# Bonus sums tied to steps of the block inverse's substitution, and a key layout in which one 128x128 transpose serves two heads

## The chip, the cores and the metric

The kernel runs on one core of a Trainium2 chip. The metric is the device time of one execution in microseconds; before the change three executions took 909.81, 911.17 and 912.35 us, median 911.17. A TensorE matmul engine (PE), VectorE (DVE), ScalarE (ACT), GpSimd (POOL) and SyncE (SP) each run a list of instructions in a fixed order and wait for each other through semaphores. ACT, POOL and SP also start DMA transfers from their lists.

## The reference

One block of a streaming encoder on 512 frames of 1024 channels, all in float32: an RWKV-7 branch and an RG-LRU branch from one input projection, merged by gates; then cross-attention into 256 memory frames; then a gated ConvFFN; RMSNorm in front of each and at the end. The change is in the RWKV-7 branch:

```python
def step(state, inp):
    r_t, w_t, k_t, v_t, a_t, b_t = inp
    sa = jnp.einsum('bhij,bhj->bhi', state, a_t)
    state = (state * w_t[:, :, None, :] + sa[..., None] * b_t[:, :, None, :]
             + v_t[..., None] * k_t[:, :, None, :])
    y_t = jnp.einsum('bhij,bhj->bhi', state, r_t)
...
y = ((y - mean) * lax.rsqrt(var + LNX_EPS)).reshape(bsz, s, A_WIDTH) * lnx_g + lnx_b
bonus = jnp.sum(r * k * r_k, axis=-1, keepdims=True) * v
return (y + bonus.reshape(bsz, s, A_WIDTH)) * g
```

There are 8 heads of 64 channels. `a_t` is minus the normalised key `kk`, and `b_t` is `kk * a`, where `a` is a sigmoid gate. The bonus of a head is a sum over its 64 channels of `r * k * r_k`, times `v`.

## The kernel before

**Precision.** A float32 weight is split into a high part (ACT copies it to a shorter format, L114) and a low part (DVE subtracts, L115), and each product is three matmuls (`mm3`, L160 to L162). `sum_exact` (L150 to L157) sums over the 64 channels of a head in the same way: ACT makes the high half, DVE the low half, and PE multiplies each by a matrix of blocks of ones into one PSUM bank.

**Staging.** Channels lie on the 128 partitions, frames along the free dimension. Two heads share a tile of 128 partitions: a pair; there are four pairs, each half of the partitions one head. The recurrence goes in 8 chunks of 64 frames.

1. The keys and values of the memory, and the norm of x, to about 57 us.
2. The input projection `in_proj` (`inproj`, L516): 38 blocks of 128 columns, 24 matmuls of 512 frames each. First the 14 blocks that RWKV-7 needs, then 24 others. From about 57 us PE takes these blocks, and what the other stages give it is put between them.
3. For each pair, between 100 and 195 us: `prep` and `prep2` make the decays, gates and normalised keys; the betas `kk*a` and the keys `k`, both divided by the running decay, are written into `KBt`; `scores` (L598) multiplies them by `AK` and masks the results into `BZ` and `AK`; the block of scores goes out to DRAM (`dM`). `bonus` (L585) forms `r*k*r_k`, sums it with `sum_exact`, multiplies by `vT`, adds the bias `lnx_b` and writes it out to DRAM (`dBo`), from where the group norm near the end of the branch reads it.
4. The inverse of a 32x32 triangular block for each head and chunk: `Nm` is loaded from `dM` on SP's queue (L654), and DVE substitutes in 31 steps (L656 to L661), each a product (L660, `zz`) and a reduction (L661, into `Zt`), from 212.45 to 253 us. The rest of the inverse follows with PE (`zh`, L687).
5. The loop over the chunks, from 285 to 343 us: `rows_kb` (L741) transposes the betas and keys of a chunk on PE, so that frames lie on the partitions, and ACT copies them out of PSUM; `chunk` (L753) uses them for the state's update.
6. Merge, cross-attention and FFN, to 900 us.

**Order.** A scheduler sets every engine's list when the kernel is built, by the priorities of the program. PE's matmuls of stage 4 and 5 are put between those of `in_proj`. A weight's raw data has four buffers, its high and low parts three each. SP's queue takes the loads of raw weights in turn, with the loads of stage 4 between them; a load waits until its buffer is free. GpSimd sums weights of the FFN in DRAM by DMA (`dS`), each of its transfers tied to a matmul of `in_proj`.

**Layout of KBt.** Each pair has 2·8 + 1 rows of 64 frames: row 1 + 2c holds the betas of chunk c for both heads, the rows after it the keys of the first head and the rows before it the keys of the second. So the 128 columns that belong together (`kb_cols`) begin at another row for each half of the partitions, and the two heads are transposed apart.

Of the kernel before, what the change touches and what calls it, by code (L numbers as in the profile page):

```python
# [53 lines left out]
def hybrid_block_kernel(ctx: ExitStack, tc: tile.TileContext, xT_d, mT_d, pv_d, cst_d, win_d, wk_d, wv_d,  # L54
# [423 lines left out]
    pa_ctx = ExitStack()  # L478
    pa = pa_ctx.enter_context(tc.tile_pool(name="pa", bufs=1, reuse_waits="tile"))
    BZ = pa.tile([P, NPAIR * NC, P], F32, tag="AR", name="BZ")  # L480
    KBt = big.tile([P, NPAIR, 2 * NC + 1, HD], F32, tag="x16", name="KBt")
    vT = pa.tile([P, NPAIR, T], F32, name="vT")
    AK = pa.tile([P, 2, NPAIR * NC, P], F32, tag="SC", name="AK")
    PC = pa.tile([P, NPAIR, NC], F32, name="PC")
# [76 lines left out]
    def prep2(j, pk, pr, at, Pi, Pp):  # L561
        c3 = lambda a: a.rearrange("p (c t) -> p c t", t=HD)
        kk = pp.tile([P, T], F32, tag="kk", name=f"kk{j}")
        S.activation(kk, pk, AF.Copy, scale=par("k_k", j))
        sq = pp.tile([P, T], F32, tag="q", name=f"sq{j}", bufs=2)
        S.activation(sq, kk, AF.Square)
        ps = rw_ps(f"ss{j}")
        sum_exact(ps, bonesr, sq, tp, "xb", f"ss{j}")
        tab.rsqrt(sq, ps, 1.0, eps[:, 2:3])
        V.scalar_tensor_tensor(kk, sq, 1e12, kk, ALU.min, ALU.mult)  # L570
        jc = slice(j * NC, (j + 1) * NC)
        for e in range(2):
            hs = half[e]
            V.scalar_tensor_tensor(AK[hs, e, jc, 0:HD], c3(kk)[hs], -1.0, Pp[hs, :, 0:HD], ALU.mult, ALU.mult)
        V.tensor_tensor(kk, kk, at, ALU.mult)
        V.tensor_tensor(KBt[:, j, 1::2, :], c3(kk), c3(Pi), ALU.mult)
        S.activation(at, at, AF.Identity, scale=par("k_a", j), bias=oka[:, j:j + 1])
        V.tensor_tensor(pk, pk, at, ALU.mult)
        V.tensor_tensor(KBt[0:HD, j, 2::2, :], c3(pk)[0:HD], c3(Pi)[0:HD], ALU.mult)
        V.tensor_tensor(KBt[HD:P, j, 0:2 * NC:2, :], c3(pk)[HD:P], c3(Pi)[HD:P], ALU.mult)  # L580
        for e in range(2):
            hs = half[e]
            V.tensor_tensor(AK[hs, e, jc, HD:P], c3(pr)[hs], Pp[hs, :, 1:], ALU.mult)

    def bonus(j, pk, pr):  # L585
        V.scalar_tensor_tensor(pr, pr, par("r_k", j), pk, ALU.mult, ALU.mult)
        ps = rw_ps(f"bo{j}")
        sum_exact(ps, bonesr, pr, tp, "xb", f"bo{j}")
        V.tensor_tensor(pr, ps, vT[:, j, :], ALU.mult)
        S.activation(pr, pr, AF.Identity, bias=par("lnx_b", j))  # L590
        nc.scalar.dma_start(dBo[j], pr)

    def kb_cols(j, e, c):
        return KBt[half[e], j, 2 * c + 1 - e:2 * c + 3 - e, :].rearrange("p a t -> p (a t)")

    def scores(j):  # L598
        for e in range(2):
            hs, oh = half[e], half[1 - e]  # L600
            for cg in range(2):
                ps = rw_ps(f"sc{j}_{e}_{cg}")
                i0 = j * NC + cg * 4
                for i in range(4):
                    PE.matmul(ps[:, i * P:(i + 1) * P], kb_cols(j, e, cg * 4 + i), AK[hs, e, i0 + i, :],
                              start=True, stop=True)
                p3 = ps.rearrange("p (c t) -> p c t", t=P)
                m3 = scmask.unsqueeze(1).to_broadcast([P, 4, P])
                V.tensor_tensor(BZ[hs, i0:i0 + 4, :], p3[hs], m3[hs], ALU.mult)
                V.tensor_tensor(AK[oh, e, i0:i0 + 4, :], p3[oh], m3[oh], ALU.mult)  # L610
            with tc.high_priority(offset=1000000):
                nc.sync.dma_start(dM[e * 32 + j * NC:e * 32 + (j + 1) * NC].rearrange("i s t -> s i t"),
                                  BZ[hs, j * NC:(j + 1) * NC, 0:HD])
# [7 lines left out]
    for jp in range(2):  # L621
        js = (2 * jp, 2 * jp + 1)
        pks, prs = {}, {}
        for j in js:
            pks[j] = pp.tile([P, T], F32, tag="pk", name=f"pk{j}", bufs=2)
            evac_shift(inproj(4 + j), 4 + j, pks[j])
        for j in js:
            prs[j] = pp.tile([P, T], F32, tag="pr", name=f"pr{j}", bufs=3)
            evac_shift(inproj(j), j, prs[j])
        for j in js:  # L630
            evac_shift(inproj(8 + j), 8 + j, vT[:, j, :])
        for j in js:
            if j == 3:
                for i in IN_REST[:NEARLY]:
                    gate_block(i - 22)
            at, L, Pp = prep(j)
            prep2(j, pks[j], prs[j], at, L, Pp)
            scores(j)
            bonus(j, pks[j], prs[j])

    pp_ctx.close()
    pq_ctx = ExitStack()
    pq = pq_ctx.enter_context(tc.tile_pool(name="pq", bufs=1, reuse_waits="tile"))
    YB = pq.tile([P, 4, T], F32, name="YB")


    with tc.tile_pool(name="pz", bufs=1, reuse_waits="tile") as pz:
        Nm = pz.tile([P, 32, 32], F32, name="Nm")
        Zt = pz.tile([P, 32, 32], F32, name="Zt")
        Zn = pz.tile([P, 32, 32], F32, name="Zn")  # L650
        zz = pz.tile([P, 31 * 31], F32, name="zz")
        with tc.high_priority(offset=1000000):
            for b in range(2):
                nc.sync.dma_start(Nm[b * HD:(b + 1) * HD], dM[:, b * 32:(b + 1) * 32, b * 32:(b + 1) * 32])  # L654
        V.memset(Zt, 0.0)
        V.memset(Zt.rearrange("p a b -> p (a b)")[:, 0:1024:33], 1.0)  # L656
        for s in range(30, -1, -1):
            n = 31 - s
            t3 = zz[:, 0:n * n].rearrange("p (a b) -> p a b", b=n)
            V.tensor_tensor(t3, Zt[:, s + 1:, s + 1:], Nm[:, s:s + 1, s + 1:].to_broadcast([P, n, n]), ALU.mult)  # L660
            V.tensor_reduce(Zt[:, s + 1:, s:s + 1], t3, AX.X, ALU.add)  # L661
        V.tensor_copy(Zn, Zt.rearrange("p a b -> p b a"))
        with tc.high_priority(offset=1000000):
            for b in range(2):
                nc.sync.dma_start(dZ[b], Zn[b * HD:(b + 1) * HD])
            nc.sync.dma_start(dZt, Zt[0:HD])
# [72 lines left out]
        return UV  # L739

    def rows_kb(c):  # L741
        KBr = ch.tile([P, 2, NPAIR, HD], F32, tag="KBr", name=f"KBr{c}", bufs=2)
        for e in range(2):
            ps = ch_ps(f"kbr{c}_{e}", ("kv", "s")[e])
            for j in range(NPAIR):
                PE.transpose(ps[:, j * HD:(j + 1) * HD], kb_cols(j, e, c), ident[half[e], half[e]])
            S.copy(KBr[:, e], j3(ps[:, 0:256]))
        return KBr

    def pc_b(c):  # L750
# [2 lines left out]
    def chunk(c, UV, KBr, SP):  # L753
# [22 lines left out]
        if not last:  # L776
            nUV = rows_v(c + 1)
            pss = ch_ps(f"s{c}", "s")
            for j in range(NPAIR):
                for e in range(2):  # L780
                    PE.matmul(pss[half[e], j * HD:(j + 1) * HD], KBr[:, e, j, :], UV[:, e, j, :],
                              start=True, stop=True)
        for j in range(NPAIR):
            for e in range(2):
# [633 lines left out]
```

## Time and profile before

| | us |
|---|---|
| median of three executions | 911.17 |
| the profiled execution | 909.73 |
| its span, from the first to the last instruction | 908.0 |
| PE busy | 890.5 (98%) |
| DVE busy | 687.4 (76%) |
| ACT busy | 510.4 (56%) |
| POOL busy | 129.3 (14%) |

The profile comes from one execution. "Busy" counts the time in which an engine runs at least one instruction; issuing a DMA does not count. In a timeline, "[0.35 <-DVE bo_l L155]" behind a row says that the engine was idle for 0.35 us before it, and that DVE's instruction of line 155 ended the wait. Matmuls overlap: the time between the starts of two in a row is less than the length of one. The granted clock of PE is 1.00 at 2.4 GHz and 0.50 at 1.2 GHz.

### The profile page before, as it was taken

To read this page: it belongs to the slowest core of one execution; us is meant where nothing else is said; L and a number is where in the kernel's file an instruction comes from. 1 tells how busy PE (TensorE), PEld (TensorE's weight loads), DVE (VectorE), ACT (ScalarE), POOL (GpSimd) and SP (SyncE) were. 2 spreads that over 40 slices of the span, in tenths; PEclk is the share of its full clock that TensorE was granted. 3 is DMA by queue.
4 is the path that set the end of the run, shared out by engine and by line. 5 is a ranking of instruction groups with operands and counts; after the bars stand their busy time and mean duration, and the time that the engine had idled before them with its cause. 6 is when DMAs were issued, how large, how long until landed. Compare 5 with 4: busy or idle time off the path is not lost. (4 is left out here: it accounts for less than half of the span.)

```text
span 908.0 us, 15914 instructions
## 1 busy us (share of the span) xinstructions
PE 890.5 (98%) x6218; PEld 776.1 (85%) x6218; DVE 687.4 (76%) x1096; ACT 510.4 (56%) x779; POOL 129.3 (14%) x159
## 2 busy tenths in 40 slices
PE   7999999999999999999999999999999999999996
PEld 6988877788877777887887778999999999999996
DVE  7884598776957585776565568788998888999674
ACT  6674675542236675234454446765665556767663
POOL 0102222010011212001112211111111111201100
PEclk9999999999999999999999999999999999999999
DMA  8878899667499749858788868898989998998963
GB/s 276 277 263 230 186 237 208 179 165 206 139 205 246 167 106 194 258 180 223 210 243 190 177 152 185 240 273 247 280 249 290 258 316 251 248 277 222 269 197 93
DMA packets 102411, 200.07 MB, mean 220 GB/s; under 512 B 25344, under 2 KB 36736, under 8 KB 102272
## 3 DMA queue, kind: packets, MB, share of 16 engines
q1 hardware_dynamic: 69504, 119.75, 41.0%
q0 software_dynamic: 25504, 67.38, 36.8%
q10 hardware_dynamic: 7328, 11.92, 3.9%
q8 instruction: 49, 0.80, 0.3%
q14 instruction: 26, 0.21, 0.1%
HBM read 187.75 MB, written 77.59 MB: 292 GB/s over the span
## 5 line engine op out<-in xcount | busy, mean ns | idle before, releaser
L126 ACT CAST wfi_h<-wfi_r 128x1024 fp32r<-128x1024 f32 x77 | 81.0, 1052 | 76.8 <-PE fx_ps L161 21.1
L160 PE MATMUL in_ps<-hT,win_h 128*128 128x512 f32 x304 | 121.9, 402 | 0.8 <-DVE pr L525 0.7
L162 PE MATMUL in_ps<-hT,win_l 128*128 128x512 f32 x304 | 120.8, 398 | 0.0
L161 PE MATMUL in_ps<-hT,win_h 128*128 128x512 f32 x304 | 120.6, 398 | 0.0
L127 DVE TENSOR_TENSOR wfi_l<-wfi_r,wfi_h 128x1024 fp32r<-128x1024 f32 x77 | 94.0, 1221 | 23.5 <-ACT wfi_h L126 23.3
L425 POOL DMA_DIRECT2D dS<-in_wfi x66 | 66.5, 1044 | 267.0 <-PE in_ps L160 132.4
L114 ACT CAST win_h<-win_r 128x1024 fp32r<-128x1024 f32 x38 | 39.8, 1048 | 71.9 <-PE in_ps L161 70.9
L115 DVE TENSOR_TENSOR win_l<-win_r,win_h 128x1024 fp32r<-128x1024 f32 x38 | 46.4, 1221 | 32.6 <-ACT win_h L114 32.5
L160 PEld LDWEIGHTS in_ps<-hT,win_h 128*128 128x128 f32 x304 | 57.0, 187 | 15.6 <-DVE pr L525 1.1
L161 PEld LDWEIGHTS in_ps<-hT,win_h 128*128 128x128 f32 x304 | 57.0, 188 | 14.0 <-issue 0.7
L162 PEld LDWEIGHTS in_ps<-hT,win_l 128*128 128x128 f32 x304 | 57.0, 187 | 13.9 <-issue 0.2
L461 POOL DMA_DIRECT2D dOs<-in_wfo x54 | 39.9, 804 | 186.0 <-PE fx_ps L160 50.9
L1245 DVE TENSOR_TENSOR wfo_l<-wfo_r,wfo_h 128x1024 fp32r<-128x1024 f32 (+1 forms) x39 | 47.2, 1210 | 13.6 <-ACT wfo_h L1244 13.5
L1244 ACT CAST wfo_h<-wfo_r 128x1024 fp32r<-128x1024 f32 (+1 forms) x39 | 40.4, 1038 | 28.2 <-PE oyz_ps L161 9.8
L161 PE MATMUL fx_ps<-hr,wfi_h 128*128 128x256 f32 x176 | 49.7, 282 | 0.0
L162 PE MATMUL fx_ps<-hr,wfi_l 128*128 128x256 f32 x176 | 49.7, 282 | 0.0
L160 PE MATMUL ox_ps<-go,wfo_h 128*128 128x256 f32 x176 | 49.6, 282 | 0.1
L160 PE MATMUL fyz_ps<-hq,wfi_h 128*128 128x256 f32 x176 | 49.3, 280 | 0.4 <-ACT p L1173 0.4
L160 PE MATMUL fx_ps<-hq,wfi_h 128*128 128x256 f32 x176 | 49.5, 281 | 0.0
L160 PE MATMUL fx_ps<-hr,wfi_h 128*128 128x256 f32 x176 | 49.4, 281 | 0.0
L162 PE MATMUL ox_ps<-go,wfo_l 128*128 128x256 f32 x176 | 49.3, 280 | 0.0
L161 PE MATMUL ox_ps<-go,wfo_h 128*128 128x256 f32 x176 | 49.3, 280 | 0.0
(418 smaller groups left out, 2727.8 us busy)
## 6 DMA issues: line engine op xcount, KB each, us to landing
dS<-in_wfi POOLq DMA_DIRECT2D x66, 512.0 KB, 8.4
wfi_r<-dS SPq DMA_DIRECT2D x44, 512.0 KB, 6.9
win_r<-in_win SPq DMA_DIRECT2D x38, 512.0 KB, 5.0
wfi_r<-in_wfi SPq DMA_DIRECT2D x33, 512.0 KB, 5.6
dS<-dS POOLq DMA_DIRECT2D x22, 512.0 KB, 5.7
dOs<-in_wfo POOLq DMA_DIRECT2D x12, 512.0 KB, 7.8
wv_r<-in_wv SPq DMA_DIRECT2D x8, 512.0 KB, 4.9
dG<-gs ACTq DMA_DIRECT2D x16, 256.0 KB, 2.6
```

The source lines that it names most:

```text
L114: S.copy(hi[:, o:o + n], raw[:, o:o + n])
L115: V.tensor_tensor(lo[:, o:o + n], raw[:, o:o + n], hi[:, o:o + n].bitcast(F32), ALU.subtract)
L126: S.copy(hi, raw)
L127: V.tensor_tensor(lo, raw, hi.bitcast(F32), ALU.subtract)
L160: first = PE.matmul(ps, lh, rh, start=start, stop=False, **kw)
L161: PE.matmul(ps, lh, rl, start=False, stop=False, **kw)
L162: PE.matmul(ps, ll, rh, start=False, stop=stop, **kw)
L425: return lambda: nc.gpsimd.dma_start(s(out), src, **kw)
L461: yield lambda k=k, w=w, src=src: nc.gpsimd.dma_start(dO[n, m][:, k * P:(k + w) * P], src, **kw)
L1244: S.copy(hi[:, :n], raw[:, :n])
L1245: V.tensor_tensor(lo[:, :n], raw[:, :n], hi[:, :n].bitcast(F32), ALU.subtract)
```

## The change

There are two edits.

**Layout.** `KBt` loses its odd row: a chunk has two rows, betas first and keys second for the first head, keys first and betas second for the second. The columns of a chunk are then the same for both halves of the partitions. DVE writes them in four pieces of 64 partitions for each pair (before: one of 128 and two of 64). `rows_kb` transposes a pair's 128x128 block at once, four transposes into one PSUM bank and one copy by ACT for each chunk (before: eight transposes of 64 partitions into two banks, two copies).

**Bonus.** `bonus` is cut in two. `bonus_terms` stays in the preparation of each pair: it makes `r*k*r_k` and writes it to DRAM. After the four pairs it is read back into four tiles (`bt`), on ACT's queue. The sum, the product with `vT` and the bias are placed in the loop of the substitution: those of pair 0, 1, 2 and 3 are tied to follow the reductions of the steps s = 20, 16, 12 and 8 (of 11, 15, 19 and 23 columns). The tie orders DVE's instructions alone; ACT's high half and PE's first matmul are free to come sooner.

```diff
--- before.py
+++ after.py
@@ -478,7 +478,7 @@
     pa_ctx = ExitStack()
     pa = pa_ctx.enter_context(tc.tile_pool(name="pa", bufs=1, reuse_waits="tile"))
     BZ = pa.tile([P, NPAIR * NC, P], F32, tag="AR", name="BZ")
-    KBt = big.tile([P, NPAIR, 2 * NC + 1, HD], F32, tag="x16", name="KBt")
+    KBt = big.tile([P, NPAIR, 2 * NC, HD], F32, tag="x16", name="KBt")
     vT = pa.tile([P, NPAIR, T], F32, name="vT")
     AK = pa.tile([P, 2, NPAIR * NC, P], F32, tag="SC", name="AK")
     PC = pa.tile([P, NPAIR, NC], F32, name="PC")
@@ -573,27 +573,33 @@
             hs = half[e]
             V.scalar_tensor_tensor(AK[hs, e, jc, 0:HD], c3(kk)[hs], -1.0, Pp[hs, :, 0:HD], ALU.mult, ALU.mult)
         V.tensor_tensor(kk, kk, at, ALU.mult)
-        V.tensor_tensor(KBt[:, j, 1::2, :], c3(kk), c3(Pi), ALU.mult)
         S.activation(at, at, AF.Identity, scale=par("k_a", j), bias=oka[:, j:j + 1])
         V.tensor_tensor(pk, pk, at, ALU.mult)
-        V.tensor_tensor(KBt[0:HD, j, 2::2, :], c3(pk)[0:HD], c3(Pi)[0:HD], ALU.mult)
-        V.tensor_tensor(KBt[HD:P, j, 0:2 * NC:2, :], c3(pk)[HD:P], c3(Pi)[HD:P], ALU.mult)
+        for e in range(2):
+            hs = half[e]
+            V.tensor_tensor(KBt[hs, j, e::2, :], c3(kk)[hs], c3(Pi)[hs], ALU.mult)
+            V.tensor_tensor(KBt[hs, j, 1 - e::2, :], c3(pk)[hs], c3(Pi)[hs], ALU.mult)
         for e in range(2):
             hs = half[e]
             V.tensor_tensor(AK[hs, e, jc, HD:P], c3(pr)[hs], Pp[hs, :, 1:], ALU.mult)
 
-    def bonus(j, pk, pr):
+    def bonus_terms(j, pk, pr):
+
         V.scalar_tensor_tensor(pr, pr, par("r_k", j), pk, ALU.mult, ALU.mult)
+        nc.scalar.dma_start(dBo[j], pr)
+
+    def bonus(j, bt):
         ps = rw_ps(f"bo{j}")
-        sum_exact(ps, bonesr, pr, tp, "xb", f"bo{j}")
-        V.tensor_tensor(pr, ps, vT[:, j, :], ALU.mult)
-        S.activation(pr, pr, AF.Identity, bias=par("lnx_b", j))
-        nc.scalar.dma_start(dBo[j], pr)
-
-
-
-    def kb_cols(j, e, c):
-        return KBt[half[e], j, 2 * c + 1 - e:2 * c + 3 - e, :].rearrange("p a t -> p (a t)")
+        sum_exact(ps, bonesr, bt, tp, "xb", f"bo{j}")
+        V.tensor_tensor(bt, ps, vT[:, j, :], ALU.mult)
+        S.activation(bt, bt, AF.Identity, bias=par("lnx_b", j))
+        nc.scalar.dma_start(dBo[j], bt)
+
+
+
+
+    def kb_cols(j, hs, c):
+        return KBt[hs, j, 2 * c:2 * c + 2, :].rearrange("p a t -> p (a t)")
 
     def scores(j):
         for e in range(2):
@@ -602,7 +608,7 @@
                 ps = rw_ps(f"sc{j}_{e}_{cg}")
                 i0 = j * NC + cg * 4
                 for i in range(4):
-                    PE.matmul(ps[:, i * P:(i + 1) * P], kb_cols(j, e, cg * 4 + i), AK[hs, e, i0 + i, :],
+                    PE.matmul(ps[:, i * P:(i + 1) * P], kb_cols(j, hs, cg * 4 + i), AK[hs, e, i0 + i, :],
                               start=True, stop=True)
                 p3 = ps.rearrange("p (c t) -> p c t", t=P)
                 m3 = scmask.unsqueeze(1).to_broadcast([P, 4, P])
@@ -636,12 +642,15 @@
             at, L, Pp = prep(j)
             prep2(j, pks[j], prs[j], at, L, Pp)
             scores(j)
-            bonus(j, pks[j], prs[j])
+            bonus_terms(j, pks[j], prs[j])
 
     pp_ctx.close()
     pq_ctx = ExitStack()
     pq = pq_ctx.enter_context(tc.tile_pool(name="pq", bufs=1, reuse_waits="tile"))
     YB = pq.tile([P, 4, T], F32, name="YB")
+    bts = [tp.tile([P, T], F32, tag=("ga", "gx")[j % 2], name=f"bt{j}", bufs=2) for j in range(NPAIR)]
+    for j in range(NPAIR):
+        nc.scalar.dma_start(bts[j], dBo[j])
 
 
     with tc.tile_pool(name="pz", bufs=1, reuse_waits="tile") as pz:
@@ -658,7 +667,10 @@
             n = 31 - s
             t3 = zz[:, 0:n * n].rearrange("p (a b) -> p a b", b=n)
             V.tensor_tensor(t3, Zt[:, s + 1:, s + 1:], Nm[:, s:s + 1, s + 1:].to_broadcast([P, n, n]), ALU.mult)
-            V.tensor_reduce(Zt[:, s + 1:, s:s + 1], t3, AX.X, ALU.add)
+            ins = V.tensor_reduce(Zt[:, s + 1:, s:s + 1], t3, AX.X, ALU.add)
+            if s % 4 == 0 and 8 <= s <= 20:
+                with tc.issue_after(ins.ins):
+                    bonus(5 - s // 4, bts[5 - s // 4])
         V.tensor_copy(Zn, Zt.rearrange("p a b -> p b a"))
         with tc.high_priority(offset=1000000):
             for b in range(2):
@@ -739,12 +751,12 @@
         return UV
 
     def rows_kb(c):
-        KBr = ch.tile([P, 2, NPAIR, HD], F32, tag="KBr", name=f"KBr{c}", bufs=2)
-        for e in range(2):
-            ps = ch_ps(f"kbr{c}_{e}", ("kv", "s")[e])
-            for j in range(NPAIR):
-                PE.transpose(ps[:, j * HD:(j + 1) * HD], kb_cols(j, e, c), ident[half[e], half[e]])
-            S.copy(KBr[:, e], j3(ps[:, 0:256]))
+
+        KBr = ch.tile([P, NPAIR, P], F32, tag="KBr", name=f"KBr{c}", bufs=2)
+        ps = ch_ps(f"kbr{c}", "kv")
+        for j in range(NPAIR):
+            PE.transpose(ps[:, j * P:(j + 1) * P], kb_cols(j, slice(0, P), c), ident)
+        S.copy(KBr, ps.rearrange("p (j i) -> p j i", i=P))
         return KBr
 
     def pc_b(c):
@@ -778,7 +790,7 @@
             pss = ch_ps(f"s{c}", "s")
             for j in range(NPAIR):
                 for e in range(2):
-                    PE.matmul(pss[half[e], j * HD:(j + 1) * HD], KBr[:, e, j, :], UV[:, e, j, :],
+                    PE.matmul(pss[half[e], j * HD:(j + 1) * HD], KBr[:, j, half[e]], UV[:, e, j, :],
                               start=True, stop=True)
         for j in range(NPAIR):
             for e in range(2):
```

DVE's list in the substitution. Before, the steps of 10 to 14 columns follow each other without anything between:

```order
L661 TENSOR_REDUCE Zt<-zz 128x11
L660 TENSOR_TENSOR zz<-Zt,Nm 128x144
L661 TENSOR_REDUCE Zt<-zz 128x12
L660 TENSOR_TENSOR zz<-Zt,Nm 128x169
L661 TENSOR_REDUCE Zt<-zz 128x13
L660 TENSOR_TENSOR zz<-Zt,Nm 128x196
L661 TENSOR_REDUCE Zt<-zz 128x14
```

The same place now (`bo_l` is the low half for the bonus sum of pair 0, `bt<-bo,vT` its product with v, `win_l` the low part of a weight of `in_proj`):

```order
L669 TENSOR_TENSOR zz<-Zt,Nm 128x121
L115 TENSOR_TENSOR win_l_2879<-win_r_2876,win_h_2878 128x1024
L670 TENSOR_REDUCE Zt<-zz 128x11
L155 TENSOR_TENSOR bo_l<-bt_1710,bo_h 128x512
L669 TENSOR_TENSOR zz<-Zt,Nm 128x144
L670 TENSOR_REDUCE Zt<-zz 128x12
L669 TENSOR_TENSOR zz<-Zt,Nm 128x169
L594 TENSOR_TENSOR bt_1710<-bo_1751,vT 128x512
L670 TENSOR_REDUCE Zt<-zz 128x13
```

Two bonus operations stand between the steps, the second behind a result of PE, and a weight's low part has come there from the step of 7 columns (`zz` 128x49).

PE's list at the bonus sums. Before, those of pair 0 to 2 stood further ahead, from block 10 of the 38 on; pair 3's two matmuls, the last, stood in block 20:

```order
L156 MATMUL bo_1727<-bo_h,bonesr 128x512
L161 MATMUL in_ps_2735<-hT_1_90,win_h_2738 128x512
L162 MATMUL in_ps_2735<-hT_0_89,win_l_2739 128x512
L160 MATMUL in_ps_2735<-hT_0_89,win_h_2738 128x512
L161 MATMUL in_ps_2735<-hT_1_90,win_h_2738 128x512
L162 MATMUL in_ps_2735<-hT_0_89,win_l_2739 128x512
L157 MATMUL bo_1727<-bo_l,bonesr 128x512
```

Now the second matmul of pair 0 and the first of pair 1:

```order
L160 MATMUL in_ps_2807<-hT_0_89,win_h_2810 128x512
L161 MATMUL in_ps_2807<-hT_1_90,win_h_2810 128x512
L157 MATMUL bo_1751<-bo_l,bonesr 128x512
L162 MATMUL in_ps_2807<-hT_0_89,win_l_2811 128x512
L156 MATMUL bo_1769<-bo_h,bonesr 128x512
L160 MATMUL in_ps_2807<-hT_0_89,win_h_2810 128x512
L161 MATMUL in_ps_2807<-hT_1_90,win_h_2810 128x512
```

The second matmul of pair 0 now stands in block 23 of the projection, 86 of its matmuls behind the begin of block 20, with more matmuls of the projection behind it. Pair 0's first stands in block 19, and pair 1's first right behind pair 0's second. The other pairs' second matmuls follow within 75 projection matmuls.

## Rows read from the trace of the kernel before

**Rows 1.** Windows: from:to, us, busy PE, PEld, DVE, ACT, POOL, clock, DMA share

```profile
100.00:195.00 95.00, 92.94 (x459) 74.27 (x458) 81.09 (x122) 58.83 (x78) 14.95 (x16) 1.00 0.80 198
195.00:262.00 67.00, 67.00 (x289) 53.63 (x288) 51.10 (x85) 20.91 (x26) 3.73 (x4) 1.00 0.65 179
262.00:345.00 83.00, 83.00 (x1200) 61.45 (x1200) 54.50 (x103) 54.95 (x101) 16.63 (x18) 1.00 0.79 173
...
904.00:908.00 4.00, 0.00 (x0) 0.00 (x0) 0.00 (x0) 0.00 (x0) 0.00 (x0) 0.50 0.62 178
```

**Rows 2.** Timeline of PE in prep (start, us, instruction, [idle before <-releaser])

```profile
144.75 0.49 PE L157 MATMUL bo<-bo_l,bonesr 128*128 128x512 f32 x1 [0.35 <-DVE bo_l L155]
```

**Rows 3.** DVE's groups between 100 and 195 (busy us, mean ns | idle)

```profile
L580 DVE TENSOR_TENSOR KBt<-pk,L 64x512 f32<-64x512 f32 x4 | 2.8, 689 | 0.1
...
L155 DVE TENSOR_TENSOR bo_l<-pr,bo_h 128x512 fp32r<-128x512 f32 x3 | 2.0, 675 | 0.0
```

**Rows 4.** Timeline of PE up to the begin of block 20 of in_proj

```profile
191.70 0.39 PE L161 MATMUL in_ps<-hT,win_h 128*128 128x512 f32 x1
...
194.96 0.39 PE L160 MATMUL in_ps<-hT,win_h 128*128 128x512 f32 x1
```

**Rows 5.** Timeline of SP's queue before the substitution (issues)

```profile
197.27 0.33 SPq L102 DMA_DIRECT2D win_r<-in_win  x1
197.78 8.65 SPq L654 DMA_DIRECT2D Nm<-dM  x2
```

**Rows 6.** Timeline of DVE before the substitution

```profile
196.01 1.23 DVE L115 TENSOR_TENSOR win_l<-win_r,win_h 128x1024 fp32r<-128x1024 f32 x1 [0.28 <-ACT win_h L114]
...
206.98 0.91 DVE L655 MEMSET Zt<- 128x1024 f32 x1 [3.62 <-DMA dBo<-pr]
...
208.01 1.23 DVE L115 TENSOR_TENSOR win_l<-win_r,win_h 128x1024 fp32r<-128x1024 f32 x1
```

**Rows 7.** Timeline of DVE in the substitution

```profile
212.45 0.16 DVE L660 TENSOR_TENSOR zz<-Zt,Nm 128x1 f32<-128x1 f32 x1 [3.22 <-DMA Nm<-dM]
...
218.42 0.28 DVE L661 TENSOR_REDUCE Zt<-zz 128x11 f32<-128x121 f32 x1
218.74 0.31 DVE L660 TENSOR_TENSOR zz<-Zt,Nm 128x144 f32<-128x144 f32 x1
...
233.58 0.70 DVE L661 TENSOR_REDUCE Zt<-zz 128x23 f32<-128x529 f32 x1
```

**Rows 8.** DMA issues between 184 and 214 (count, KB each, us to landing)

```profile
Nm<-dM SPq DMA_DIRECT2D x2, 256.0 KB, 13.7
...
dBo<-pr ACTq DMA_DIRECT2D x1, 256.0 KB, 6.7
```

**Rows 9.** Timeline of PE in the chunk loop

```profile
301.94 0.22 PE L734 MATMUL vr<-cst,vT 64*64 64x64 f32 x1
302.09 0.46 PE L746 MATMUL kbr<-cst,KBt 64*128 64x64 f32 x4
302.48 0.69 PE L734 MATMUL vr<-cst,vT 64*64 64x64 f32 x12
```

**Rows 10.** Timeline of PE at the scores of pair 0

```profile
115.25 3.50 PE L605 MATMUL sc<-AK,KBt 64*128 64x128 f32 x32
```

**Rows 11.** Timeline of DVE at the substitution's end

```profile
253.11 1.12 DVE L662 COPY Zn<-Zt 128x1024 f32<-128x1024 f32 x1
```

**Rows 12.** Timeline of PE at the first matmuls with the inverse

```profile
266.45 1.19 PE L687 MATMUL zh<-ZA,BZ 32*32 32x32 f32 x32
```

**Rows 13.** Timeline of PE at the end of the run

```profile
899.74 0.71 PE L1299 MATMUL rs_ps<-t,ones 128*128 128x128 f32 x4 [0.28 <-ACT t L1289]
```

**Rows 14.** Timeline of PE in its first ten microseconds and just behind

```profile
6.20 0.58 PE L160 MATMUL k_ps<-m,wk_h 128*128 128x256 f32 x1 [6.20 <-ACT m L286]
...
15.81 0.40 PE L161 MATMUL k_ps<-m,wk_h 128*128 128x256 f32 x1
...
16.40 0.28 PE L162 MATMUL k_ps<-m,wk_l 128*128 128x256 f32 x1
```


## The prediction

> **What bounds the kernel now.** I read the windows by stage first [rows 1]. From 100 to 195 us, where the keys, scores and bonus sums of the four head pairs are made between the blocks of the input projection, TensorE (PE) is busy for 92.94 of 95 us. From 195 to 262 and from 262 to 345 it is busy without a gap. VectorE (DVE) has 81.09 of 95 us in the first of these and a quarter to a third free in the other two; ScalarE (ACT) has more. So PE's list of instructions sets the end: an edit counts if it shortens that list or changes a wait of PE. Next I read PE's timeline for the idle time that is there: row [rows 2] is one of the waits, 0.35 us before the second bonus matmul of a pair, ended by the low half that DVE makes for it. All of them together are 95.00 − 92.94 = 2.06 us, the bonus sums of the early pairs and the evictions in front of prep among them. In the windows after 195 there is none to win. Last I read the places to which work moves: DVE's timeline of the substitution and the loads in front of it [rows 5 to 8], and PE's in the chunk loop [rows 9].
>
> **The bonus sums leave prep.** Removed from prep for each pair: two ACT operations, the low half and the product with vT on DVE, two PE matmuls. The matmuls are only moved: 0.233 us each at the pace of PE's list (14 of the projection's from 191.70 to 194.96, 3.26 us) [rows 4], eight of them, net 0. What may go are PE's waits: between 0 and 2.06 us. I take 1.5, because the waits fall where DVE has its longest run of work per pair, and the bonus' part of that run goes, while waits on evictions (they are in the 2.06 too) need not. On DVE prep loses two operations for each pair, the low half at 0.68 us [rows 3] and the product with vT, of the same size and taken at the same, and gains one, below, so it ends a little earlier or as before. What is late next there is ACT's and DVE's work for the next pair, already in the list.
>
> **Keys written in four 64-row pieces instead of three.** The 64x512 piece takes 0.689 us [rows 3], four of these 2.8 us more DVE work, in a stage where DVE has 95 − 81.09 = 13.9 us free. I take 0. Without that cover it would stand before the scores, at most 0.69 us per pair, 2.8 in all; the two operations that leave pay for it.
>
> **The wait that comes.** In the new order PE meets the second matmul of pair 0 (on bo_l) in block 23 of the projection, 86 matmuls after block 20 begins. T is the begin of block 20, 194.96 before [rows 4]. At 0.233 us each PE is there at T + 20.0. On DVE bo_l stands behind the reduction of 11 columns of the substitution. When is that? Before, the substitution's first product starts at 212.45, T + 17.5, released by the load of Nm [rows 7]. That load is issued on SP's queue behind a weight load that waits for a weight buffer [rows 5]; the buffer comes free with the low half that starts at 196.01, 1.05 us behind T, itself released by ACT's cast and that by PE [rows 6]. The load thus keeps its distance to PE, not to DVE. So I leave the start at T + 17.5. From there to the start of the 11th reduction it is 218.42 − 212.45 = 5.97 us, with one split of a weight (win_l) in it; after too there is one in it, moved to just before that reduction. The reduction takes 0.28 [rows 7], bo_l 0.68 [rows 3]. bo_l is ready at T + 17.5 + 5.97 + 0.28 + 0.68 = T + 24.4, PE waits 24.4 − 20.0 = 4.4 us. Nothing overtakes it: PE's list is fixed, and the projection's matmuls stand behind bo_l.
>
> The later three bonus sums: from 218.74 to the reduction of 23 columns, ending at 234.28, DVE needs 15.5 us [rows 7]; with six bonus operations (six times 0.68 less the gaps between, some 3.7) 19.2. PE has 75 projection matmuls and six bonus ones in the same stretch, 81 × 0.233 = 18.9. So 0.3 us more, in all 4.7.
>
> Bounds. Below: the load of Nm took 13.7 us for two pieces of 256 KB while another, dBo's 256 KB, took 6.7 [rows 8]; the first is long, and pair 3's dBo goes to another time. But the chain can't start before the split of the weight that stands in front of it, 208.01 + 1.23 = T + 14.3 [rows 6]; 3.2 us earlier, the wait is 1.2. That split stood behind two memsets that waited for a landing of dBo; without them it can follow its weight some 0.6 earlier, so 0.6. Above: ACT issues a read of dBo of pair 3 behind its write, and waits for that landing before it makes the next high half of a weight. If that takes 6.7 us [rows 8], DVE's split and with it Nm and the chain may come 2.1 us later: 6.8. I take 4.7, from the rows as they stand.
>
> **The transposes.** Before, each of the eight chunks has two runs of four, 64 rows by 128 columns of weights, into two banks; now one run of four 128x128 and one copy. A run takes 302.48 − 302.09 = 0.39 us, and entering it costs 0.15 where the steps of its neighbours are 0.05 (301.94 to 302.09, and twelve in 0.69) [rows 9]: 0.10. Eight entries go: −0.8. If a merged run takes what a run took, eight runs of 0.39 go as well: −3.1. If it takes twice as long, because twice as many columns are streamed, nothing: 0. The nearest row with 128 columns behind 64x128 weights, the scores, has 3.50/32 = 0.109 us per matmul [rows 10], 0.44 a run, close to 0.39 and far from 0.78. So the whole is −3.9, its bounds −3.9 and −0.8. The chunk loop is a stretch in which PE is without a gap [rows 1], so this comes off the end in full. ACT's second copy goes, off the path.
>
> **The rest of the substitution.** It grows by four bonus sums on DVE, eight operations, about 4.9 us. It ended before when Zn was written, 253.11 + 1.12 [rows 11], and PE meets the first matmul with the inverse at 266.45 [rows 12]: 12.2 us to spare, and PE itself comes 4.7 us later. Hidden. The eight more DMAs (four reads of dBo, four second writes, 256 KB each) fall where the DMA engines are busy 0.65 of the time [rows 1]; priced at 0 but for the case above.
>
> **Sum.** −1.5 + 4.7 − 3.9 = −0.7. The profiled execution took 909.73 (span 908.0, 1.73 around it); 909.0 in its terms. The median of the runs, 911.17, lies 1.44 above it: 910.5.
>
> **Rivals.**
> *The clock falls in the wait (slower).* At the end of the run PE's last matmuls end at 899.74 + 0.71 = 900.45, and from 904 on the granted clock is 0.50, the lower of its two levels (1.2 GHz) [rows 13, 1]; the half-microsecond waits of prep left it at 1.00 [rows 2, 1]. A wait of about 4 us on bo_l lies nearer the first. It decides if that wait is of that size and not about 1 us. The price: matmuls go at half pace for a while, and lose half of it. At the start, first matmul at 6.20, 256-column matmuls take 0.40 until 15.81 and 0.28 from 16.40 [rows 14]; some 9.8 us at half pace lose 4.9. The shorter bound is a stretch like 900.45 to 904, 3.55 us, losing 1.8. Sum −0.7 + 1.8 … 4.9 = +1.1 … +4.2: 912.3 to 915.4, middle 913.8. Against it: the granted clock is 1.00 in [rows 1] for every stage with waits. The Trainium skill, "TensorE: Matmul & The Clock Gate", section "HAM oscillation — how this bites in real kernels", says that an idle gap between bursts of matmuls brings the engine back to its half clock, so that the next burst starts cold. By that rule the wait costs once more than itself; the trace agrees at its end and has no gap of such length inside.
>
> *Nm lands early (faster).* The write of pair 3's dBo no longer goes out behind block 20, at the time of Nm's load. The chain then starts at its floor, T + 14.3, the wait is 1.2: −0.7 − 3.2 = −3.9, 907.3. For it: 13.7 us is long for its 256 KB beside 6.7 [rows 8]; against it: the reads of bt, four of the same size, come at the same time.
>
> *Prep's waits stay.* The DVE run of a pair keeps its length, one operation more and two less, and the wait goes from bo_l to the eviction behind it. Then −0.7 + 1.5 = +0.8: 912.0.
>
> **How the numbers follow.** Forecast 0.48, own range 907.5 to 913; clock 0.20; early Nm 0.20; prep 0.12. 0.3% is 2.7 us, about what a measurement of this kernel can tell from no change. Faster by more, under 908.4: 0.14 of early Nm's 0.20, 0.08 of the forecast's own range where the wait is near its lower bound, 0.22 in sum. Slower, over 913.9: 0.11 of the clock's, 0.06 of the forecast's (transposes near −0.8 or the wait near 6.8), 0.04 of prep's: 0.21. The rest, 0.57, within. Range: the low end is −2.06 + 0.6 − 3.9 = −5.4, with 911.17 that is 905.8, put at 905.5; at the high end the wait's bound alone gives −0.7 + 2.1 = +1.4 and the clock up to +4.2, of which the last half a microsecond and the meetings of several bounds, about 1 in 10, are left out: 915.0.
>
> **What would show it.** A PE row for the second bonus matmul (bo_l) about 20 us after block 20 begins, with some 4 us of idle time ended by DVE's bo_l, and hardly any at the other three. Idle time of PE between 100 and 195 well under 2 us. A transposing run of four of about 0.39 us, eight of them. The granted clock in the microseconds after the wait: 1.00 for the forecast, under it for the first rival. The start of the first zz against T: 17.5 for the forecast, near 14.3 for the second rival. It is wrong if the wait is nowhere near 4 us, if the merged runs take 0.78, or if a new wait stands at the first matmul with the inverse.

## The result and the profile after

Over 22 executions of each, the kernel before takes 910.27 us in the median and the changed one 913.14; the ratio is 1.0026, its 95% interval [1.0014, 1.0037]. So it is 1.3 to 3.4 us slower, where 0.7 us faster was forecast. The profiled execution has a span of 912.1 us (before: 908.0) and a mean clock of 0.994.

The windows of the stages, in the order of [rows 1]:

```profile
100.00:195.00 95.00, 93.60 (x462) 75.24 (x461) 82.03 (x121) 56.63 (x74) 16.13 (x17) 1.00 0.81 209
195.00:262.00 67.00, 63.04 (x259) 50.00 (x258) 49.46 (x85) 20.87 (x27) 1.14 (x1) 0.95 0.62 171
262.00:345.00 83.00, 82.98 (x1154) 62.01 (x1153) 55.02 (x103) 54.16 (x90) 17.58 (x19) 1.00 0.86 188
```

PE's busy time in prep rises from 92.94 to 93.60 us. From 195 to 262 it falls from 67.00 to 63.04: there is a hole of 3.96 us that was not there, and the mean clock is 0.95. PE's timeline shows the hole in one piece, ahead of the second bonus matmul of pair 0, and behind it matmuls that start 0.43 us apart instead of 0.23:

```profile
216.64 0.79 PE L157 MATMUL bo<-bo_l,bonesr 128*128 128x512 f32 x1 [3.96 <-DVE bo_l L155]
217.24 0.63 PE L162 MATMUL in_ps<-hT,win_l 128*128 128x512 f32 x1
...
221.50 0.63 PE L162 MATMUL in_ps<-hT,win_l 128*128 128x512 f32 x1
221.93 0.50 PE L160 MATMUL in_ps<-hT,win_h 128*128 128x512 f32 x1
222.27 0.40 PE L161 MATMUL in_ps<-hT,win_h 128*128 128x512 f32 x1
222.50 0.39 PE L162 MATMUL in_ps<-hT,win_l 128*128 128x512 f32 x1
...
223.20 0.40 PE L157 MATMUL bo<-bo_l,bonesr 128*128 128x512 f32 x1
...
229.27 0.40 PE L157 MATMUL bo<-bo_l,bonesr 128*128 128x512 f32 x1
```

The windows of the same stretch (columns as above; the third number from the end is the granted clock):

```profile
215.00:217.00 2.00, 0.36 (x1) 0.36 (x2) 1.97 (x5) 0.38 (x1) 0.00 (x0) 0.58 0.21 23
217.00:221.00 4.00, 4.00 (x10) 3.07 (x10) 3.81 (x10) 0.96 (x2) 0.00 (x0) 0.50 0.50 185
221.00:222.00 1.00, 1.00 (x4) 0.73 (x3) 0.00 (x0) 0.26 (x1) 0.00 (x0) 0.50 0.00 0
222.00:223.00 1.00, 1.00 (x6) 0.82 (x5) 0.18 (x1) 1.00 (x2) 0.00 (x0) 0.92 0.00 0
```

From 216.64 to 222.27 there are 13 steps; at 0.233 they would take 3.03 us, they take 5.63. The half clock costs 2.6 us. The second matmuls of pairs 1 and 2 (223.20, 229.27) have no wait. DVE's timeline shows what the hole waited for; these rows answer to [rows 7]:

```profile
209.76 0.16 DVE L669 TENSOR_TENSOR zz<-Zt,Nm 128x1 f32<-128x1 f32 x1 [3.83 <-DMA Nm<-dM]
...
214.38 0.29 DVE L669 TENSOR_TENSOR zz<-Zt,Nm 128x121 f32<-128x121 f32 x1
214.59 1.22 DVE L115 TENSOR_TENSOR win_l<-win_r,win_h 128x1024 fp32r<-128x1024 f32 x1
215.72 0.27 DVE L670 TENSOR_REDUCE Zt<-zz 128x11 f32<-128x121 f32 x1
215.91 0.68 DVE L155 TENSOR_TENSOR bo_l<-bt,bo_h 128x512 fp32r<-128x512 f32 x1
```

Block 20 of the projection begins at T = 192.46 here, by PE's timeline (194.96 before):

```profile
192.46 0.40 PE L160 MATMUL in_ps<-hT,win_h 128*128 128x512 f32 x1
```
The substitution starts when Nm has landed, at T + 17.3; `bo_l` starts at T + 23.5, PE goes on at T + 24.2. What SP's queue waited for between 190 and 200 (total, times, longest) shows what holds the load of Nm (L663) back:

```profile
SPq L663 <- DMA dM<-BZ: 1.6, 1, 1.6
SPq L102 <- DVE win_l L115: 1.2, 1, 1.2
```

It waits 1.6 us for the scores' write to DRAM (dM), behind a weight load that waits 1.2 us for its buffer. The chunk loop's transposes, in answer to [rows 9]:

```profile
305.77 0.66 PE L758 MATMUL kbr<-cst,KBt 128*128 128x128 f32 x4
```

A run of four now takes 0.66 us from first start to last end, where four of the old ones took 0.46. Added up over all starts in the trace, PE gives 6.50 us to the transposes before and 4.03 after.

Where the 4.1 us between the two profiled executions lie, from the starts on PE. "Up to T" leaves out five bonus matmuls that now come later (1.2 us); the first matmul with the inverse starts at 272.89 (before: 266.45 [rows 12]).

| stretch | us |
|---|---|
| memory's keys and values, to 57 us | −0.4 |
| projection and prep, up to T | −0.9 |
| the hole at `bo_l` | +4.1 |
| the half clock behind it | +2.6 |
| rest of substitution and chunk loop | −2.3 |
| behind 360 us | +1.0 |

The hole counts 4.1 in this table, since it is taken from start to start. The first and the last line are places that the change doesn't touch; the first goes from −1.2 to +1.2 in the other executions of this study.

### The profile page after: what moved, and what is told of

Its sections match the earlier page's. It is cut to its first block, busy times and chain, and to the rows that moved or that the text cites. A ratio compares the mean times of both kernels' runs of the same rounds, so it can differ in the third digit from the quotient of the medians.

```text
span 912.1 us, 15864 instructions
## 1 busy us (share of the span) xinstructions
PE 889.7 (98%) x6186; PEld 775.5 (85%) x6186; DVE 690.4 (76%) x1100; ACT 509.8 (56%) x771; POOL 129.5 (14%) x159
## 4 chain that ended last, share of the span: by engine, by line
PE 85%; DVE 6%; DMA 6%; ACT 1%; issue 1%; SPq 0%; POOL 0%; DVEq 0%; ACTq 0%
PE in_ps L160 7%; PE in_ps L161 7%; PE in_ps L162 7%; PE fx_ps L161 5%; PE fx_ps L160 5%; PE fx_ps L162 5%; PE fyz_ps L161 3%; PE fyz_ps L162 3%; PE fyz_ps L160 3%; DMA wfo_r<-dOs 2%; PE co_ps L161 2%; PE mix_ps L160 2%; PE mix_ps L161 2%; PE co_ps L160 2%; PE mix_ps L162 2%; PE co_ps L162 2%
## 5 line engine op out<-in xcount | busy, mean ns | idle before, releaser
L127 DVE TENSOR_TENSOR wfi_l<-wfi_r,wfi_h 128x1024 fp32r<-128x1024 f32 x77 | 94.0, 1221 | 23.4 <-ACT wfi_h L126 23.3
L162 PEld LDWEIGHTS in_ps<-hT,win_l 128*128 128x128 f32 x304 | 57.6, 189 | 13.9 <-issue 0.2
L1257 DVE TENSOR_TENSOR wfo_l<-wfo_r,wfo_h 128x1024 fp32r<-128x1024 f32 (+1 forms) x39 | 47.1, 1207 | 15.3 <-ACT wfo_h L1256 13.9
L160 PE MATMUL ox_ps<-go,wfo_h 128*128 128x256 f32 x176 | 49.7, 282 | 0.0
L162 PE MATMUL fx_ps<-hq,wfi_l 128*128 128x256 f32 x176 | 49.3, 280 | 0.0
```

Of the source, the lines that this page charges most:

```text
L127: V.tensor_tensor(lo, raw, hi.bitcast(F32), ALU.subtract)
L160: first = PE.matmul(ps, lh, rh, start=start, stop=False, **kw)
L162: PE.matmul(ps, ll, rh, start=False, stop=stop, **kw)
L1257: V.tensor_tensor(lo[:, :n], raw[:, :n], hi[:, :n].bitcast(F32), ALU.subtract)
```

## The experiments

**Theory A:** the loss is PE's wait at the first bonus sum and the half clock behind it; layout and prep gain about 3 us. **Rivals:** the layout gains nothing (B); the DMAs or DVE's longer list cost the time (C). In all diffs the base is the changed kernel if nothing else is said.

**The edits alone.** `e1_layout` is the kernel before with the layout edit of the diff above, `e2_bonus` with the bonus edit.

> The layout edit alone: keys and betas in two rows per chunk, one 128x128 transpose per pair; the bonus sums stay in the preparation of the pairs as before. Theory A (the loss is the wait of PE at the first bonus sum plus the half clock behind it, and the layout gains): about -2.5 us against the kernel before (PE's transposes took 6.50 us of PE's list before and 4.03 in the changed kernel), ratio 0.997; no PE wait over 1 us between 195 and 262. Rival B (the four DVE pieces of the keys delay prep and eat the gain): 0 to +1, with PE's idle time between 100 and 195 above the 2.06 us of before.

> The bonus edit alone, in the key layout of before. Theory A: wait about 4.1 us at the second bonus matmul of pair 0, then about 12 projection matmuls at 0.43 instead of 0.233 us (2.5 us), prep 0.9 shorter: +5.7 us, ratio 1.006. Rival B: the bonus edit costs about 2.4 us, what the whole change cost, because the layout gains nothing.

Measured: layout alone 910.92 us, ratio 1.0010 [0.9993, 1.0026]; bonus alone 919.32, ratio 1.0093 [1.0076, 1.0110]. Neither is what theory A said. The layout alone came out as rival B had it; the bonus edit alone cost more than either had said. PE's timelines show why; first the layout alone, its waits over 1.5 us:

```profile
130.07 0.50 PE L160 MATMUL in_ps<-hT,win_h 128*128 128x512 f32 x1 [1.83 <-DVE pk L525]
...
147.03 0.50 PE L156 MATMUL bo<-bo_h,bonesr 128*128 128x512 f32 x1 [1.87 <-ACT bo_h L154]
...
474.31 0.39 PE L1017 MATMUL sc_ps<-K,q 128*128 128x256 f32 x1 [2.40 <-ACT ex L1024]
```

The transposes take 4.35 us here, so the gain of 2.2 is there. In this execution (912.27 us, the median is 910.92) it is lost to two waits in prep (PE's idle time from 100 to 195 is 4.25 us, before 2.06) and one in the attention stage, where nothing of the change is. Eight of the 12 executions have a mean clock of 0.995 or 0.996, below the 0.998 of this one, so they lose part of the gain to a half clock. That DVE's four pieces make the waits in prep, as rival B has it, is not shown: the changed kernel has the same pieces, and 1.40 us of idle time there. Behind the wait in the attention stage stands ACT, which waits for a load of keys:

```profile
469.72 1.05 ACT L995 CAST K<-kvK 128x1024 fp32r<-128x1024 f32 x1 [3.38 <-DMA kvK<-dK]
```

The bonus edit alone has the hole at the bonus sum, and two further waits:

```profile
150.71 0.50 PE L156 MATMUL ss<-ss_h,bonesr 128*128 128x512 f32 x1 [1.76 <-ACT ss_h L154]
...
217.85 0.57 PE L157 MATMUL bo<-bo_l,bonesr 128*128 128x512 f32 x1 [3.38 <-DVE bo_l L155]
...
477.51 0.57 PE L1027 MATMUL sc_ps<-K,q 128*128 128x256 f32 x1 [1.88 <-ACT ex L1034]
```

A second profile of this kernel (the run's label, e6_bonus_nm_in_four, names a load in four pieces that it does not have) asked whether they are chance.

> The bonus edit alone once more, for a second profile: it lost 8.5 us where theory A expected 5.7; its profile had waits of 1.9 us in prep and 2.0 us in the attention stage beside the 3.5 us at the bonus sum. If these belong to its lists, they stand at the same two places again; if they are chance of one execution, elsewhere or not at all.

```profile
151.34 0.51 PE L156 MATMUL ss<-ss_h,bonesr 128*128 128x512 f32 x1 [1.84 <-ACT ss_h L154]
...
220.38 0.50 PE L157 MATMUL bo<-bo_l,bonesr 128*128 128x512 f32 x1 [3.75 <-DVE bo_l L155]
```

918.26 us. The waits in prep and at the bonus sum stand again at the same places; that of the attention stage is down to 0.44 us. Two of the three belong to the lists.

**Where the wait comes from.** `e3_early` takes the bonus sums out of the substitution:

```diff
+    for j in range(NPAIR):
+        bonus(j, bts[j])
...
-            if s % 4 == 0 and 8 <= s <= 20:
-                with tc.issue_after(ins.ins):
-                    bonus(5 - s // 4, bts[5 - s // 4])
```

> The changed kernel with the four bonus sums ahead of the substitution and not tied to its steps (terms still through DRAM): in PE's list they stand in blocks 19.8 to 21.2 of the projection instead of 23.6 to 26.7. Theory A: no wait over 1 us behind 195, clock 1.00, so the changed kernel less 4.1 and 2.5: about -4 against the kernel before, ratio 0.996. Rival C (the longer list of DVE's work or the eight more transfers cost the time, not the wait): no better than the changed kernel, +2.

It came out slower than the kernel before and the changed one: 917.12 us, ratio 1.0066 [1.0051, 1.0082]. Theory A was wrong about it. The execution that was profiled took 2210.9 us (the other five 915.40 to 917.26), so a second look was taken, with a new expectation:

> The kernel with the bonus sums ahead of the substitution once more, for its profile alone: it was 6 us slower than the kernel before where theory A expected 4 us faster. The bonus sums leave DVE's list of the substitution, and the scheduler puts the first matmul with the inverse in block 32.0 of the projection instead of 32.5. Theory A' (the list again places a matmul before the load of Nm lets it be ready, now that one): a PE wait of 3 to 6 us at the first zh matmul and a clock of 0.50 behind it. Rival C (more transfers or DVE work): no wait over 2 us, the loss spread.

```profile
272.58 1.91 PE L698 MATMUL zh<-ZA,BZ 32*32 32x32 f32 x32 [8.47 <-DMA ZA<-dZt]
```

The hole has moved to the first matmul with the inverse and is 8.47 us long, where 3 to 6 were expected; the clock is 0.50 from 273 to 276. The place in the list explains little of it: block 32.0, where the changed kernel has 32.5 and the kernel before 32.3. PE gets there at T + 70.6, about as before (T + 71.5), since it loses nothing at the bonus sums. What comes late is the load of ZA. The substitution's result goes through DRAM (`dZt`, `dZ`) and comes back as ZA; its issues on SP's queue and its landings (count, KB each, median us to landing), in the kernel before and then here, where T is 193.51:

```profile
258.53 2.75 SPq L676 DMA_DIRECT2D ZA<-dZt  x2
ZA<-dZt SPq DMA_DIRECT2D x2, 128.0 KB, 7.3
```

```profile
264.54 2.65 SPq L687 DMA_DIRECT2D ZA<-dZt  x2
ZA<-dZt SPq DMA_DIRECT2D x2, 128.0 KB, 8.8
```

The first piece of ZA lands at T + 70.6 before, 0.9 us ahead of PE; at T + 75.1 in the changed kernel, where PE comes at T + 80.4; and at T + 79.0 here. The substitution itself ends 3.2 us earlier than in the changed kernel, though Nm takes up to 16.8 us to land (there 11.8). Behind it the write `dZ` takes 7.0 us (there 3.9) and ZA 8.8 (there 6.3). Why these same transfers land later here was not settled, so this run does not decide against rival C.

`e4_nm_in_four` moves PE's matmul instead, through the load that the scheduler plans with:

```diff
-            for b in range(2):
-                nc.sync.dma_start(Nm[b * HD:(b + 1) * HD], dM[:, b * 32:(b + 1) * 32, b * 32:(b + 1) * 32])
+            for b, r0, r1 in ((0, 0, 32), (0, 32, 64), (1, 0, 32), (1, 32, 64)):
+                nc.sync.dma_start(Nm[b * HD + r0:b * HD + r1], dM[r0:r1, b * 32:(b + 1) * 32, b * 32:(b + 1) * 32])
```

> The changed kernel with the load of Nm in four pieces instead of two, same bytes, same queue. The scheduler then puts PE's second bonus matmul of pair 0 in block 24.25 of the projection instead of 23.58, 16 matmuls = 3.7 us later; DVE's order of bonus sum and steps stays. Theory A1 (the wait is the difference between where the list puts the matmul and when Nm lands on the chip): wait about 0.4 us if Nm lands as before, no fall of the clock, -4 us against the kernel before, ratio 0.996. Rival A2 (the wait belongs to the bonus sum's place behind the 11th step, whatever the list): wait again about 4 us and a clock of 0.50 behind it, +2.

907.59 us, ratio 0.9972 [0.9958, 0.9986]: faster than both kernels. PE waits about 0.3 us at the bonus sum and 0.36 at the inverse, and the clock stays:

```profile
195.00:262.00 67.00, 66.86 (x286) 53.05 (x285) 53.98 (x91) 22.88 (x30) 3.06 (x4) 1.00 0.64 182
```

```profile
217.20 0.40 PE L162 MATMUL in_ps<-hT,win_l 128*128 128x512 f32 x1
217.74 0.51 PE L157 MATMUL bo<-bo_l,bonesr 128*128 128x512 f32 x1
```

Two things moved, though: PE's list by 16 matmuls (3.7 us), and the start of the substitution, now T + 15.4 (209.08) instead of T + 17.3, since the first piece of Nm no longer waits for the second write of dM. The earlier start does not reach `bo_l`, though: a weight split that waits 1.67 us for ACT has come into the chain, and `bo_l` starts at 217.00, T + 23.4 (changed kernel: T + 23.5). So it was the list that took the wait away, 3.7 of its 4.1 us. And as the bonus sums on DVE and the bytes moved are those of the changed kernel, rival C is not what that one loses. The next runs move the two apart. `e9_later_steps` ties each sum four steps later:

```diff
-            if s % 4 == 0 and 8 <= s <= 20:
+            if s % 4 == 0 and 4 <= s <= 16:
...
-                    bonus(5 - s // 4, bts[5 - s // 4])
+                    bonus(4 - s // 4, bts[4 - s // 4])
```

> The changed kernel with each bonus sum tied four steps later (to the reductions of 15, 19, 23 and 27 columns). PE's list then has the second bonus matmul of pair 0 in block 24.08 instead of 23.58, 12 matmuls = 2.8 us later; DVE reaches it about 2.6 us later as well. Theory A1 (the list is made for a load of Nm that lands some 4 us sooner than the chip's): the wait stays, 3.5 to 4.5 us, the clock falls to 0.50 behind it, and the time is that of the changed kernel, ratio 1.002 to 1.003. Rival A2 (the wait comes from tying the sum too early in the chain): the later tie takes most of it away, 907 to 909.

912.95 us, ratio 1.0020 [1.0006, 1.0034]. The wait is there with 3.56 us, since PE's list moved as far as DVE's; A2 falls.

```profile
219.03 0.80 PE L157 MATMUL bo<-bo_l,bonesr 128*128 128x512 f32 x1 [3.56 <-DVE bo_l L155]
219.63 0.63 PE L162 MATMUL in_ps<-hT,win_l 128*128 128x512 f32 x1
...
222.19 0.44 PE L161 MATMUL in_ps<-hT,win_h 128*128 128x512 f32 x1
```

`e10_nm_in_three` cuts only the first piece in halves: `((0, 0, 32), (0, 32, 64), (1, 0, 64))`.

> The changed kernel with one of Nm's two pieces cut in halves (three pieces). PE's second bonus matmul of pair 0 stands in block 23.62, one matmul later than in the changed kernel, so only the landing can move the wait. Theory A1: the wait follows the landing one for one: 2.0 us if Nm lands at 15.3 us behind block 20's begin (as with four pieces), 3.9 if at 17.2 (as with two). Theory K (the half clock is an item of its own, besides the wait): if the clock falls, about 12 projection matmuls at 0.43 us, 2.4 us, whatever the wait; rival K0 (the slow stretch costs in proportion to the wait): half as many at half the wait.

911.52 us, ratio 1.0004 [0.9990, 1.0018]. PE's matmul is where it was, the substitution starts at T + 15.3, and the wait is 1.70 us, where 2.0 were expected for this start:

```profile
216.31 0.50 PE L157 MATMUL bo<-bo_l,bonesr 128*128 128x512 f32 x1 [1.70 <-DVE bo_l L155]
216.65 0.39 PE L160 MATMUL in_ps<-hT,win_h 128*128 128x512 f32 x1
```

The steps behind it are 0.23 us: no half clock in this execution. So the wait is set by two things, PE's place in its list and the landing, as A1 says. (What landing the scheduler counts with is in no trace; that it is earlier than the chip's is concluded from e4, e9 and e10.) And wait and half clock are two items; how the second grows with the first (K or K0) this run doesn't tell, as it did not come.

**Controls.** `e8_before_nm4` is the kernel before with the load in four pieces, `e7_bonus_nm4` the bonus edit in the layout of before with it.

> The kernel before with nothing changed but the load of Nm in four pieces. Control: if the pieces are worth something by themselves, this is faster than before too. Theory A: it removes no wait of the kernel before (PE has none between 195 and 262), so 0, ratio 0.999 to 1.001. Rival N (the pieces gain 3 to 5 us whatever the bonus sums do): ratio 0.995 to 0.997.

> The bonus edit in the key layout of before, with the load of Nm in four pieces: no wait at the bonus sum in either this or the changed kernel with the load in four pieces, so the two differ by the layout alone. Theory L (the layout is worth the PE time of its transposes, 6.50 - 4.03 us): 2.5 us slower than the changed kernel with the load in four pieces, 0 against the kernel before, ratio 1.000. Rival L0 (the layout gains nothing on the chip, as the layout alone showed +0.9): the same time as that kernel, ratio 0.997.

The pieces alone: 912.44 us, ratio 1.0030 [1.0007, 1.0053]; they are no gain by themselves, and not the 0 of theory A either. Their profile has a new wait of 1.45 us at the inverse, with a clock of 0.50 behind it. With the bonus edit: 913.24, ratio 1.0035 [1.0015, 1.0055], 0.63% or 5.7 us above `e4_nm_in_four`, which differs by the layout alone; L said 2.5. Between the two profiled executions lie 6.3 us. From block 20 to 360 us, where the transposes are (6.62 and 4.01 us in the traces), it is 2.1; in prep it is 4.4, one wait that the other kernel does not have and a clock of 0.50 behind it:

```profile
152.59 0.49 PE L156 MATMUL ss<-ss_h,bonesr 128*128 128x512 f32 x1 [3.16 <-ACT ss_h L154]
```

So L is right about the transposes in these lists, but not about the time, and the two edits are not additive. What the transposes take depends on the list, too. In `e2_bonus`, whose layout is the old one, they take 4.91 us and not 6.50: in four of its chunks the two runs of four stand next to each other, and all eight transposes then take what one run took, here 0.41 us up to the next matmul at 308.24. Against such a list the new layout would gain 0.9 us.

```profile
307.83 0.47 PE L757 MATMUL kbr<-cst,KBt 64*128 64x64 f32 x8
```

Why prep waits in `e7_bonus_nm4` for ACT's high half of the norm sum (`ss_h`) and does not with both edits was not settled.

**A version for use?** `e11_nm_in_five` cuts the last quarter of Nm in halves once more.

> A version for use: the changed kernel with Nm's load in five pieces. PE's second bonus matmul of pair 0 goes to block 24.62 and the first matmul with the inverse to 33.54 (with four pieces 24.25 and 33.08), 9 to 11 matmuls later. Theory A1: the last waits there, 0.3 at the bonus sum and 0.5 at the inverse, go as well: 0.5 to 1 us faster than four pieces, ratio to the kernel before 0.996. Rival E (the chunk loop now begins so late that too few projection matmuls are left to cover it): as fast or 1 to 2 us slower than four pieces, with waits behind 345 us.

917.72 us, ratio 1.0060 [1.0039, 1.0080], slower. The bonus sum has no wait left. But the inverse is 3.61 us late, and the clock is at 0.50 there:

```profile
278.63 1.91 PE L699 MATMUL zh<-ZA,BZ 32*32 32x32 f32 x32 [3.61 <-DMA ZA<-dZt]
```

DVE's list now has one more weight split ahead of the substitution, which starts at 212.30 (T + 19.0), but ends only 0.8 us later against T than in `e4_nm_in_four`. More is lost behind it: another split stands ahead of Zn's copy (1.0 us), and `dZ` and ZA take 7.5 and 10.5 us to land, there 5.5 and 9.1. A wait of 2.14 us at 371 us is of the kind that rival E named; the loss is larger than its 1 to 2 us.

`e4_nm_in_four` stays the best: 0.28% below the kernel before, and by the two ratios about 0.5% below the changed one.

## Why the prediction was wrong

- *The wait at the first bonus sum* was right in place and size: 4.4 us forecast, 3.96 measured (4.1 from start to start); the substitution started at T + 17.3 (17.5), `bo_l` let PE go at T + 24.2 (24.4). That the distance held is in part luck. Nm's load was issued at T + 4.7 (before: T + 2.8), since it waits 1.6 us for the write of dM as well, which the reasoning did not have; and its second piece landed 11.8 us behind its issue, not 13.9 as before. The two cancel. In `e5_early_look` it took 16.8.
- *The later three sums*: no wait of PE (0.3 forecast).
- *The clock* is the step that failed. The sum held it at 1.00 and gave its fall to a rival at 0.20. It stood at 0.50 from 217 to 222 us and cost 2.6 us, between the rival's bounds of 1.8 and 4.9. The argument against the rival, that every stage with waits had a clock of 1.00, rested on waits of at most 0.67 us behind 57 us. Nor is it chance of one execution: the mean clock of the 22 is 0.993 to 0.997, in 21 of them at most 0.996, where 20 of the 23 executions of the kernel before that ran beside `e1_layout` have 0.997 or 0.998. The rival's 912.3 to 915.4 holds the 913.14 measured, with some luck: two other terms of its sum, transposes and prep, were 2.0 us too good together. The Trainium skill, "TensorE: Matmul & The Clock Gate", section "HAM oscillation — how this bites in real kernels", says that an idle gap makes the next burst start cold; the rows at 217 to 222 agree.
- *The transposes* were mis-sized: −3.9 forecast, −2.5 measured. A merged run takes longer than a run of 64 rows (4.03/8 = 0.50 us against 6.50/16 = 0.41), nearer to the scores' 0.44 that was at hand than to the 0.39 taken. The step into a run, 0.15 us before as now, is not in these sums; that the entries saved gained the 0.8 us forecast does not show in the stretch, which gained 2.3 in all.
- *Prep's waits*: −1.5 forecast, −0.9 measured (PE's idle time from 100 to 195 fell from 2.06 to 1.40 us). That four pieces for three cost nothing held in this kernel; in the layout alone prep had 2.2 us more idle time.
- *The rest of the substitution* stayed hidden, but not for the reason given. The 12.2 us to spare were counted from the end of Zn's copy; the matmul waits for ZA, which comes back through DRAM, and before the change that landed 0.9 us ahead of PE. It lands 4.5 us later against T in the changed kernel, and PE had lost 6.7 us at the bonus sum by then. With that loss gone the wait is there: 0.36 us in `e4_nm_in_four`, 8.47 in `e5_early_look`, 3.61 in `e11_nm_in_five`.

With the measured sizes the sum is −0.9 + 4.1 + 2.6 − 2.3 = +3.5 us, from one execution of each kernel; the 22 executions give 1.3 to 3.4. The half clock can account for that: the profiled execution's mean clock is 0.994, the median of the 22 is 0.995, and 0.001 of 912 us stands, by estimate, for 0.9 us of work lost at half pace. That would make it +2.6.

## What to carry to other kernels

Where engines' lists are fixed ahead, an edit that ties work to a chain behind a load can make a busy engine wait for the difference between planned and real landing. Look for the first instruction in its list that needs the chain, and compare its place with the landing in a trace, before looking at how long the new work takes. Then do the same for the next instruction that needs the chain, up to the load that it really waits for: the inverse, with 0.9 us to spare and not 12.2, was the next limit. A wait in a saturated TensorE costs its length and may cost the clock as well: price both. And with such a scheduler the parts of a change can't be tested by adding them: the bonus edit costs 8.5 us alone and the layout 0.9, both together 2.4, as each edit has its own lists, and with them other waits.

## What the runs showed of the hardware

Whether the clock falls is not told by the length of the wait alone. Behind 57 us, each of the seven waits of PE of 3.16 us or more in these profiles came with a granted clock of 0.50, during the wait or within 2 us behind it. Below that it went both ways, down to the 1.45 us of `e8_before_nm4`, behind which it fell. The two executions of the bonus edit alone have the same wait at the same place in prep, 1.76 and 1.84 us. In the first the clock stays, in the second it falls some 1.8 us behind the wait's end:

```profile
152.00:153.00 1.00, 1.00 (x6) 0.81 (x5) 1.00 (x2) 0.98 (x3) 0.53 (x1) 1.00 0.27 86
153.00:154.00 1.00, 1.00 (x6) 0.82 (x5) 0.53 (x1) 1.00 (x1) 0.63 (x1) 1.00 0.14 27
154.00:156.00 2.00, 2.00 (x11) 1.59 (x10) 1.15 (x3) 1.96 (x4) 0.73 (x1) 1.00 0.77 253
```

```profile
152.00:153.00 1.00, 0.93 (x4) 0.80 (x5) 0.74 (x2) 1.00 (x3) 0.00 (x0) 1.00 0.35 133
153.00:154.00 1.00, 1.00 (x5) 0.76 (x4) 1.00 (x2) 0.98 (x2) 0.90 (x1) 0.59 0.17 55
154.00:155.00 1.00, 1.00 (x4) 0.81 (x3) 0.16 (x1) 0.99 (x2) 0.27 (x1) 0.50 0.42 61
```

In the attention stage 2.40 us in `e1_layout` left it at 1.00, and 1.88 us at the same place of `e2_bonus` brought it to 0.50:

```profile
473.00:475.00 2.00, 0.69 (x5) 0.69 (x6) 1.95 (x7) 1.00 (x3) 0.00 (x0) 1.00 1.03 157
475.00:479.00 4.00, 4.00 (x25) 3.04 (x23) 2.32 (x10) 1.62 (x6) 0.24 (x1) 1.00 0.86 278
```

```profile
477.00:478.00 1.00, 0.49 (x2) 0.49 (x3) 1.00 (x5) 0.60 (x3) 0.00 (x0) 0.78 0.94 154
478.00:480.00 2.00, 2.00 (x10) 1.82 (x9) 0.98 (x5) 0.68 (x3) 0.00 (x0) 0.50 1.08 230
```

The slow stretch differs in length too: 13 steps in the changed kernel, 7 in `e9_later_steps`, behind waits of 3.96 and 3.56 us.
